# Sum of absolute differences by row: loads on one queue, absolute sums on ScalarE, last row in pieces

## Chip, cores and metric

The kernel runs on one core of a Trainium2 chip. The metric is the device time of one execution in microseconds (us), the median of three runs.

## What is computed

`x` and `y` are float32 matrices of 1024 rows and 4096 columns (16.78 MB each). The output holds, for each row, the sum over the columns of the absolute differences:

```python
def reference(x, y, axis):          # axis = -1
    return np.sum(np.abs(x - y), axis=axis).astype(np.float32)
```

## The kernel before

The 1024 rows are dealt to the 128 partitions, eight consecutive rows to each (`(p k) c -> p k c`). One step of the loop (line 29, `KCS = [1]*8`) takes one row of every partition: a tile `tx` of 128x4096 and a tile `ty` of the same shape, 2 MB each. In the text such a step is called a row, rows 0 to 7. Each step has four instructions:

- line 33: SP's queue loads `tx` from `x`; line 34: ScalarE's queue loads `ty` from `y`. ScalarE does nothing else.
- line 35: VectorE subtracts `ty` from `tx` in place.
- line 36: VectorE sums the absolute values of `tx` into one column of `ro` (128x8).

At the end line 38 stores `ro` (4 KB) on SP's queue. The pools `px1` and `py1` have four buffers each, so the first four rows are loaded at once, and the load of row k+4 waits until VectorE has finished with row k. The order of VectorE's instructions is set by the scheduler of the framework, not by the source: it often puts the subtractions of two rows ahead of their two sums (rows 1 and 2, 3 and 4, 5 and 6).

Of the kernel before, what the change touches and what calls it, by code (L numbers as in the profile page):

```python
# [5 lines left out]

KCS = [1]*8

@with_exitstack
def kernel(ctx, tc, x, y, axis, out):  # L10
    nc = tc.nc
    P = nc.NUM_PARTITIONS
    R, C = x.shape
    K = R // P
    xr = x.rearrange("(p k) c -> p k c", p=P, k=K)
    yr = y.rearrange("(p k) c -> p k c", p=P, k=K)
    orr = out.rearrange("(p k) -> p k", p=P, k=K)
    kcs = KCS
    assert sum(kcs) == K
    pools = {}  # L20
    for kc in set(kcs):
        pools[kc] = (
            ctx.enter_context(tc.tile_pool(name=f"px{kc}", bufs=4)),
            ctx.enter_context(tc.tile_pool(name=f"py{kc}", bufs=4)),
        )
    with tc.tile_pool(name="pr", bufs=1) as poolr:
        ro = poolr.tile([P, K], mybir.dt.float32)
        o = 0
        for kc in kcs:
            poolx, pooly = pools[kc]  # L30
            tx = poolx.tile([P, kc, C], x.dtype)
            ty = pooly.tile([P, kc, C], y.dtype)
            nc.sync.dma_start(out=tx, in_=xr[:, o:o+kc, :])
            nc.scalar.dma_start(out=ty, in_=yr[:, o:o+kc, :])  # L34
            nc.vector.tensor_sub(out=tx, in0=tx, in1=ty)  # L35
            nc.vector.reduce_sum(out=ro[:, o:o+kc], in_=tx, axis=mybir.AxisListType.X, apply_absolute_value=True)  # L36
            o += kc
        nc.sync.dma_start(out=orr, in_=ro)


# [1 line left out]
_INS = ['x', 'y', 'axis']  # L42
_OUTS = [((1024,), 'float32')]
#: Inputs that are plain numbers.
_NUMBERS = {'axis': -1}


def kernel(**inputs):
    import numpy as _np
    import concourse.bacc as _bacc  # L50
    import concourse.tile as _tile
    from concourse import mybir as _mybir
    from concourse.bass_utils import run_bass_kernel_spmd as _run

    nc = _bacc.Bacc("TRN2", target_bir_lowering=False, num_devices=1)  # L55
    arrays, args = {}, []
    for name in _INS:
        if name in _NUMBERS:
            args.append(_NUMBERS[name])
            continue  # L60
        a = _np.ascontiguousarray(inputs[name])
        if a.dtype.kind in "iu":
            a = a.astype(_np.int64)
        arrays[f"in_{name}_dram"] = a
        args.append(nc.dram_tensor(f"in_{name}_dram", a.shape, _mybir.dt.from_np(a.dtype), kind="ExternalInput").ap())
    for i, (shape, dtype) in enumerate(_OUTS):
        dt = _mybir.dt.from_np(_np.dtype(dtype))
        args.append(nc.dram_tensor(f"out_{i}_dram", shape, dt, kind="ExternalOutput").ap())
    with _tile.TileContext(nc) as tc:
        kernel(tc, *args)  # L70
    r = _run(nc, [arrays], core_ids=[0])
    got = tuple(r.results[0][f"out_{i}_dram"] for i in range(len(_OUTS)))
    return got[0]
```

## Time and profile before

| what | us |
|---|---|
| median of three runs (lowest, highest) | 97.6 (97.56, 97.62) |
| span of the profiled execution, first to last instruction | 95.8 |
| median less span: what lies around the span | 1.8 |
| VectorE busy in the span | 69.9 |

The profile is of one execution and gives its span; for the time of a run, what lies around the span has to be added. All times in the views are microseconds from the start of the span. The views used further down are the page's busy times and its forty slices, the table by stretches of time, the waits, the timeline, the chain that ended last, the groups of instructions and the transfers with their time from issue to landing.

### The profile page before, as it was taken

To read this page: it belongs to the slowest core of one execution; us is meant where nothing else is said; L and a number is where in the kernel's file an instruction comes from. 1 tells how busy PE (TensorE), PEld (TensorE's weight loads), DVE (VectorE), ACT (ScalarE), POOL (GpSimd) and SP (SyncE) were. 2 spreads that over 40 slices of the span, in tenths; PEclk is the share of its full clock that TensorE was granted. 3 is DMA by queue.
4 is the path that set the end of the run, shared out by engine and by line. 5 is a ranking of instruction groups with operands and counts; after the bars stand their busy time and mean duration, and the time that the engine had idled before them with its cause. 6 is when DMAs were issued, how large, how long until landed. Compare 5 with 4: busy or idle time off the path is not lost.

```text
span 95.8 us, 95 instructions
## 1 busy us (share of the span) xinstructions
DVE 69.9 (73%) x16; POOL 0.2 (0%) x4
## 2 busy tenths in 40 slices
DVE  0000069996930499999982999999909999999990
POOL 0000000000000000000000000000000000000000
DMA  4899999999999999999999999999999995000000
GB/s 109 369 431 424 424 438 438 438 431 438 431 424 438 424 417 431 431 411 431 438 438 424 431 431 431 424 424 424 431 411 438 438 438 212 0 0 0 0 0 2
DMA packets 2448, 33.56 MB, mean 350 GB/s; under 512 B 400, under 2 KB 400, under 8 KB 400
## 3 DMA queue, kind: packets, MB, share of 16 engines
q1 hardware_dynamic: 1296, 16.78, 41.7%
q10 hardware_dynamic: 1152, 16.78, 41.1%
HBM read 33.55 MB, written 0.00 MB: 350 GB/s over the span
## 4 chain that ended last, share of the span: by engine, by line
DMA 68%; DVE 24%; issue 4%; ACTq 1%
DMA ty<-in_y_dram 68%; DVE tx L35 14%; DVE ro L36 10%; ACTq L34 1%
## 5 line engine op out<-in xcount | busy, mean ns | idle before, releaser
L35 DVE TENSOR_TENSOR tx<-tx,ty 128x4096 f32<-128x4096 f32 x8 | 35.4, 4422 | 23.6 <-DMA ty<-in_y_dram 23.6
L36 DVE TENSOR_REDUCE ro<-tx 128x1 f32<-128x4096 f32 x8 | 35.1, 4413 | 0.1
L55 POOL MEMSET const-bfloat16-1.0<- 128x1 bf16 x1 | 0.1, 103 | 0.0
L55 POOL MEMSET const-uint8-127<- 128x1 uint8 x1 | 0.1, 103 | 0.0
L55 POOL MEMSET const-float32-1.0<- 128x1 f32 x1 | 0.1, 100 | 0.0
L55 POOL MEMSET const-float32-0.0<- 128x1 f32 x1 | 0.1, 99 | 0.2 <-issue 0.2
## 6 DMA issues: line engine op xcount, KB each, us to landing
ty<-in_y_dram ACTq DMA_DIRECT2D x8, 2048.0 KB, 33.1
tx<-in_x_dram SPq DMA_DIRECT2D x8, 2048.0 KB, 23.6
out_dram<-ro SPq DMA_DIRECT2D x1, 4.0 KB, 1.4
```

Of the source, the lines that this page charges most:

```text
L34: nc.scalar.dma_start(out=ty, in_=yr[:, o:o+kc, :])
L35: nc.vector.tensor_sub(out=tx, in0=tx, in1=ty)
L36: nc.vector.reduce_sum(out=ro[:, o:o+kc], in_=tx, axis=mybir.AxisListType.X, apply_absolute_value=True)
L55: nc = _bacc.Bacc("TRN2", target_bir_lowering=False, num_devices=1)
```

## The change

- All loads are issued by SP, x before y, row by row (lines 39 and 40). There are six buffers for x and six for y.
- Row 7 is loaded in four pieces of columns, `PIECES = [2304, 1152, 512, 128]`, each piece with a load of x and one of y (lines 44 and 45).
- For rows 0 to 6 VectorE subtracts (line 50) and ScalarE takes the absolute value and, in the same instruction, its sum into `ro` (line 51).
- For row 7, VectorE subtracts piece by piece (line 64), and ScalarE writes the absolute sums of the first three pieces to three columns of a small tile `last` (line 65). The difference of the last piece, 128 columns, is written beside these into `last` (line 67), and one VectorE sum over 131 columns gives row 7's result (line 68).
- The program runs in the order in which it is written (`manual_schedule`).

```diff
-KCS = [1]*8
+PIECES = [2304, 1152, 512, 128]
...
+    px = ctx.enter_context(tc.tile_pool(name="px", bufs=6))
+    py = ctx.enter_context(tc.tile_pool(name="py", bufs=6))
+    ps = ctx.enter_context(tc.tile_pool(name="ps", bufs=1))
+    with tc.manual_schedule():
+        ro = ps.tile([P, K], F32, tag="ro")
+
+        last = ps.tile([P, n_part + PIECES[-1]], F32, tag="last")
+        tiles = []
+
+        def load(k):
+            tx = px.tile([P, C], F32, tag="tx")
+            ty = py.tile([P, C], F32, tag="ty")
+            tiles.append((tx, ty))
+            if k < K - 1:
+                nc.sync.dma_start(out=tx, in_=xr[:, k, :])
+                nc.sync.dma_start(out=ty, in_=yr[:, k, :])
+                return
+            o = 0
+            for w in PIECES:
+                nc.sync.dma_start(out=tx[:, o:o + w], in_=xr[:, k, o:o + w])
+                nc.sync.dma_start(out=ty[:, o:o + w], in_=yr[:, k, o:o + w])
+                o += w
+
+        def whole(k):
+            tx, ty = tiles[k]
+            nc.vector.tensor_sub(out=tx, in0=tx, in1=ty)
+            nc.scalar.activation(tx, tx, ABS, accum_out=ro[:, k:k + 1])
+
+        for k in range(4):
+            load(k)
+        for k in range(K - 1):
+            if k + 4 < K:
+                load(k + 4)
+            whole(k)
+        tx, ty = tiles[K - 1]
         o = 0
-        for kc in kcs:
-            poolx, pooly = pools[kc]
-            tx = poolx.tile([P, kc, C], x.dtype)
-            ty = pooly.tile([P, kc, C], y.dtype)
-            nc.sync.dma_start(out=tx, in_=xr[:, o:o+kc, :])
-            nc.scalar.dma_start(out=ty, in_=yr[:, o:o+kc, :])
-            nc.vector.tensor_sub(out=tx, in0=tx, in1=ty)
-            nc.vector.reduce_sum(out=ro[:, o:o+kc], in_=tx, axis=mybir.AxisListType.X, apply_absolute_value=True)
-            o += kc
+        for i, w in enumerate(PIECES):
+            s = slice(o, o + w)
+            if i < n_part:
+                nc.vector.tensor_sub(out=tx[:, s], in0=tx[:, s], in1=ty[:, s])
+                nc.scalar.activation(tx[:, s], tx[:, s], ABS, accum_out=last[:, i:i + 1])
+            else:
+                nc.vector.tensor_sub(out=last[:, n_part:n_part + w], in0=tx[:, s], in1=ty[:, s])
+                nc.vector.reduce_sum(out=ro[:, K - 1:K], in_=last, axis=AX, apply_absolute_value=True)
+            o += w
         nc.sync.dma_start(out=orr, in_=ro)
```

The end of VectorE's program before: two subtractions, two sums, then row 7's subtraction and sum (L35 is the subtraction, L36 the sum; x2 are two in a row, of different rows).

```order
L35 TENSOR_TENSOR tx<-tx,ty 128x4096 x2
L36 TENSOR_REDUCE ro<-tx 128x1 x2
L35 TENSOR_TENSOR tx<-tx,ty 128x4096
L36 TENSOR_REDUCE ro<-tx 128x1
L69 UNCONDITIONAL_BRANCH
```

And the whole of VectorE's program in the change:

```order
L50 TENSOR_TENSOR tx<-tx,ty 128x4096 x7
L64 TENSOR_TENSOR tx<-tx,ty 128x2304
L64 TENSOR_TENSOR tx<-tx,ty 128x1152
L64 TENSOR_TENSOR tx<-tx,ty 128x512
L67 TENSOR_TENSOR last<-tx,ty 128x128
L68 TENSOR_REDUCE ro<-last 128x1
L101 UNCONDITIONAL_BRANCH
```

Nothing but subtractions stands ahead of row 7's pieces, and one sum behind them.

ScalarE's program, as one difference: eight loads of y go, a table load and ten activations come.

```order
-L34 DMA ty<-in_y_dram 128x4096 x8
-L69 UNCONDITIONAL_BRANCH
+L101 UNCONDITIONAL_BRANCH
+L51 ACT_TABLE_LOAD
+L51 ACTIVATE tx,ro<-tx 128x4096 x7
+L65 ACTIVATE tx,last<-tx 128x2304
+L65 ACTIVATE tx,last<-tx 128x1152
+L65 ACTIVATE tx,last<-tx 128x512
+L101 UNCONDITIONAL_BRANCH
```

The last three activations are those of row 7's first three pieces, behind the activation of row 6.

The end of SP's program in the change, from row 6's loads on, with the semaphores that each load waits for (DMAHW0 to DMAHW7 are given to the loads in turn, so a load waits for the one eight places ahead of it; Activation is ScalarE, DVE is VectorE):

```order
L39 DMA tx<-in_x_dram 128x4096 [waits DMAHW4_49,Activation_49]
L40 DMA ty<-in_y_dram 128x4096 [waits DMAHW5_49,DVE_49]
L44 DMA tx<-in_x_dram 128x2304 [waits DMAHW6_49,Activation_49]
L45 DMA ty<-in_y_dram 128x2304 [waits DMAHW7_49,DVE_49]
L44 DMA tx<-in_x_dram 128x1152 [waits DMAHW0_49]
L45 DMA ty<-in_y_dram 128x1152 [waits DMAHW1_49]
L44 DMA tx<-in_x_dram 128x512 [waits DMAHW2_49]
L45 DMA ty<-in_y_dram 128x512 [waits DMAHW3_49]
L44 DMA tx<-in_x_dram 128x128 [waits DMAHW4_49]
L45 DMA ty<-in_y_dram 128x128 [waits DMAHW5_49]
L70 DMA out_dram<-ro 128x8 [waits DMAHW6_49,DVE_49]
```

Before, SP issued eight loads of x and the store; now 22 loads and the store stand in one line.

## Rows read from the trace of the kernel before

**Rows 1.** The page: busy time by engine, and the DMA engines in forty slices.

```profile
span 95.8 us, 95 instructions
...
DVE 69.9 (73%) x16; POOL 0.2 (0%) x4
...
DVE  0000069996930499999982999999909999999990
...
DMA  4899999999999999999999999999999995000000
```

**Rows 2.** Stretches: start:end, length, DVE busy, POOL busy, PEclk, DMA share, GB/s.

```profile
0.00:2.00 2.00, 0.00 (x0) 0.20 (x4) 1.00 0.57 131
60.00:70.00 10.00, 9.51 (x3) 0.00 (x0) 1.00 1.00 424
70.00:75.00 5.00, 3.30 (x1) 0.00 (x0) 1.00 1.03 436
79.00:80.00 1.00, 1.00 (x1) 0.00 (x0) 1.00 1.00 426
80.00:81.00 1.00, 1.00 (x2) 0.00 (x0) 1.00 0.29 115
81.00:82.00 1.00, 1.00 (x1) 0.00 (x0) 1.00 0.00 0
```

**Rows 3.** The waits: engine, line, what for, us in total, times, longest.

```profile
DVE tx L35 <- DMA ty<-in_y_dram: 23.6, 5, 12.9
```

**Rows 4.** Timeline: start us, us, engine, line, operation, what it waited for.

```profile
12.92 4.43 DVE L35 TENSOR_TENSOR tx<-tx,ty 128x4096 f32<-128x4096 f32 x1 [12.92 <-DMA ty<-in_y_dram]
...
32.51 4.43 DVE L35 TENSOR_TENSOR tx<-tx,ty 128x4096 f32<-128x4096 f32 x1 [5.37 <-DMA ty<-in_y_dram]
...
71.70 4.43 DVE L35 TENSOR_TENSOR tx<-tx,ty 128x4096 f32<-128x4096 f32 x1 [2.19 <-DMA ty<-in_y_dram]
76.04 8.74 DVE L36 TENSOR_REDUCE ro<-tx 128x1 f32<-128x4096 f32 x2
84.70 4.42 DVE L35 TENSOR_TENSOR tx<-tx,ty 128x4096 f32<-128x4096 f32 x1
89.15 4.42 DVE L36 TENSOR_REDUCE ro<-tx 128x1 f32<-128x4096 f32 x1
93.60 0.35 SPq L38 DMA_DIRECT2D out_dram<-ro  x1
```

**Rows 5.** The chain that ended last, its last pieces: start us, us, what.

```profile
36.97 34.71 DMA ty<-in_y_dram
71.68 0.02 issue
71.70 4.43 DVE tx L35
76.13 5.22 DVE ro L36 x2
81.34 3.36 issue
84.70 4.43 DVE tx L35
89.13 0.02 issue
89.15 4.42 DVE ro L36
```

**Rows 6.** Groups of instructions: line, engine, operation, count, busy us, mean ns, idle before.

```profile
L35 DVE TENSOR_TENSOR tx<-tx,ty 128x4096 f32<-128x4096 f32 x8 | 35.4, 4422 | 23.6 <-DMA ty<-in_y_dram 23.6
L36 DVE TENSOR_REDUCE ro<-tx 128x1 f32<-128x4096 f32 x8 | 35.1, 4413 | 0.1
L55 POOL MEMSET const-uint8-127<- 128x1 uint8 x1 | 0.1, 103 | 0.0
```

**Rows 7.** Timeline of the start: the first four loads of each queue.

```profile
0.72 2.05 ACTq L34 DMA_DIRECT2D ty<-in_y_dram  x4
0.73 1.88 SPq L33 DMA_DIRECT2D tx<-in_x_dram  x4
```

**Rows 8.** The page's transfers: issues, KB each, median us from issue to landing; and queues.

```profile
q1 hardware_dynamic: 1296, 16.78, 41.7%
q10 hardware_dynamic: 1152, 16.78, 41.1%
...
ty<-in_y_dram ACTq DMA_DIRECT2D x8, 2048.0 KB, 33.1
tx<-in_x_dram SPq DMA_DIRECT2D x8, 2048.0 KB, 23.6
out_dram<-ro SPq DMA_DIRECT2D x1, 4.0 KB, 1.4
```

15 lines of the change are left out of this document (5 added, 10 removed).

## The prediction

> **What bounds the kernel now.** I began with the page's busy times and slices [rows 1]. VectorE is busy for 73% of the span, the DMA row reads 9 from the third slice to the 33rd and then drops to 0, while VectorE's row reads 9 to the end. So there are two stages: one in which the loads set the pace, and a tail in which VectorE works alone. The table by stretches [rows 2] gives the border: the DMA share is 1.00 at 424 GB/s between 60 and 70 us, still 1.00 between 79 and 80, 0.29 in the next microsecond, then 0.00.
>
> In the first stage VectorE waits for data: 23.6 us in five waits, all for y [rows 3]. The timeline [rows 4] shows the pace. Subtractions that start straight from such a wait start at 32.51 (row 2) and 71.70 (row 6), four rows apart: (71.70 - 32.51) / 4 = 9.80 us for each pair of 2 MB tiles. From row 0, at 12.92, six steps of 9.80 also give 71.7. Row 7's pair, which VectorE did not wait for, therefore lands at 71.70 + 9.80 = 81.50; that is an estimate, and it fits the stretch in which the DMA share falls to zero.
>
> The tail is the last piece of the chain [rows 5]. At 81.50 VectorE still owes the sums of rows 5 and 6, which its order put ahead of row 7's subtraction. That one starts at 84.70, 3.20 us after its data, and then come its 4.43 and the last sum's 4.42, to 93.57. From there to the end of the span, 95.8, are 2.23 us: the store's issue, its landing and the end of the program. The runs' median lies 1.8 above the profiled span, and I add that to every span below. A difference over 0.2% (0.2 us) counts as a difference.
>
> **The change part by part.**
>
> *The stream of loads.* The same 33.55 MB go through the same engines, at a share that is already 1.00. I keep 9.80 us a row and 71.70 as row 6's landing. Four SP issues take 1.88 us [rows 7], some 0.47 each; 22 of them need 10.3 us of SP's time in 81.5. The deeper buffers gain nothing, because no stretch between the start and 80 us shows engines without work. SP's line has one new danger: each load waits for the one eight places ahead of it. The last one, y's 128 columns, waits for y of row 6, which lands at 71.70. Its own turn in the stream comes at about 81.2, so 9.5 us cover an issue of 0.5. The waits on ScalarE ahead of rows 6 and 7 are for rows 0 and 1, done some 20 us earlier. If this cover were gone, the delay would go straight onto the last landing. Moving the y loads off ScalarE's queue costs nothing and keeps them from standing behind activations.
>
> *The sums that leave VectorE.* Eight sums of 4.41 us go [rows 6], 35.1 us in all. Six of them lay beside the loads and gain nothing. VectorE's subtraction of row 6 then ends at 71.70 + 4.43 = 76.13, and VectorE is free for row 7's pieces.
>
> *Row 7 in pieces.* By columns, 9.80 us split into 5.51, 2.76, 1.22 and 0.31: the pieces land at 77.21, 79.97, 81.19 and 81.50. A subtraction costs 4422 ns / 4096 = 1.08 ns a column [rows 6]. For a small operation's fixed part I add 0.10, the time of the 128x1 operation on POOL, the nearest small one [rows 6]. That gives 2.59, 1.34, 0.65 and 0.24 us. They run 77.21 to 79.80, 79.97 to 81.31, 81.31 to 81.96, and 81.96 to 82.20. The final sum over 131 columns is another 0.24.
>
> *The sums on ScalarE.* No row shows an activation, so I bound its price. At one end ScalarE is so quick that it is never last: the final sum then starts at 82.20 and ends at 82.44, the span at 84.67, the time is 86.5. At the other end it takes what VectorE takes for its sum of the same shape, 4.41 us for 4096 columns, in practice the subtraction's figures: row 6 from 76.15 to 80.57, then the pieces, 2.59, 1.34 and 0.65, one behind the other, to 85.15. The final sum ends at 85.39, the span at 87.62, the time is 89.4. ScalarE thus becomes the last link for any price but a very low one, since row 6's activation ends close to the last landing and 3968 columns wait behind it. Nothing in the rows decides between the ends, which lie 2.9 us apart; I take the middle, **88.0 us**, a gain of 9.6. Both ends stay in the range.
>
> The Trainium skill (ScalarE: Activation LUTs, section on the table load's cost) states 186 ns plus 0.833 ns an element for an activation. By that the passes would be 3.60, 2.11, 1.15 and 0.61 us, the last would end at 83.7, and the time would be 88.0 as an estimate; no row here shows it yet.
>
> The table load at the head of ScalarE's program is covered by the first landing and subtraction: the first activation can't start before 12.92 + 4.43 = 17.35 [rows 4].
>
> **The rivals.**
>
> *One queue does not stream (the other side).* If the engines drained one transfer of a queue before they began the next, each of the 21 boundaries between 22 transfers would cost a bubble. The gain of 9.6 is used up at 9.6 / 21 = 0.46 us a boundary; above that the change is slower. A cold start is dear: in the first 2 us the engines ran at 131 GB/s [rows 2], and row 0 was ready at 12.92, 3.1 us later than a pair needs in the stream. With 0.6 us a boundary, a fifth of this, 12.6 us would come on top: 100.6. In its mild form, 0.1 a boundary, the time is 90.1. For it: before, two queues always had work, 41.7% and 41.1% of the engines' span [rows 8], and one could fill the other's gap, so no row shows a queue alone. Against it: each queue had up to four transfers in flight, the one queue now has eight, and with the engines at a share of 1.00 nothing suggests that they wait for a transfer to be confirmed. I give 0.12 to the mild form and 0.03 to the dear one.
>
> *Small pieces do not stream.* The only small transfer in the trace, the store of 4 KB, took 1.4 us from issue to landing [rows 8]. If the last two pieces of 64 KB took 1.4 each, instead of 0.31 together, the last landing would be at 81.19 + 2.80 = 83.99. The last subtraction and the final sum would follow to 84.47, the time would be 88.5: the loads would be last, with ScalarE close beside. If all eight pieces put 1.4 on top of the stream, 11.2 us, the landing would be at 92.7 and the time at 97.2, hardly faster than before. For it: row 7 has 512-byte runs at its end. Against it: the pieces are issued ahead, so their way from issue to landing overlaps, and only what a small run costs an engine is left. Chance 0.05. The Trainium skill (DMA: Bandwidth & Descriptors, table of measured sizes) speaks against such pieces: it asks for 1 MiB or more and gives 0.95 us for 64 KB. Two such at the end would put the last landing at 83.1, an estimate, with a time of 87.6 by the loads' own path, which a ScalarE of the middle price covers; no row shows it.
>
> *ScalarE is slower than VectorE.* At r times VectorE's price its four last passes take 9.00 r us, and the time is 80.42 + 9.00 r. That is 91.2 at 1.2, and it passes the old time at 1.91, where a row takes 8.4 us. Since even then a row fits into the 9.80 of its loads, only the tail would show it. No row speaks for or against. Chance 0.05, nearly all below 1.91.
>
> **How the numbers follow.** My forecast (tail set by ScalarE, between 86.5 and 89.4) has 0.75. The range runs from 86.5, where ScalarE is hidden, to 90.0: it takes in the forecast's own spread, the low form of the small pieces, a ScalarE up to 6% slower than VectorE and about half of the mild bubbles. About 0.15 is left out, nearly all above. Faster by over 0.2%: 0.96. Slower: 0.03, the dear bubbles with a little of the slow ScalarE. Within 0.2%: 0.01, for the crossing points of these.
>
> **What would show it.** Right: the last landing near 81.5, subtractions of rows 0 to 6 that each wait for y and start about 9.8 apart, no idle time between the last activations, the final sum released by ScalarE and not by a load, and some 2.2 us behind it. The chain should be loads, one subtraction, four activations, the sum, the store. The pace of rows 0 to 6 tells the queue's part: over 9.80, and the first rival is at work. A gap between the subtractions of the last pieces with landings after 82 would be the second. ScalarE's mean for 128x4096 fixes the middle: 4.4 means 89.4, about 3.6 means 88. The forecast is wrong if the final sum ends before 82.4 or after 85.4, or if loads last beyond 82.5.

## The result and the profile after

The changed kernel takes 88.3 us, against 97.6 before: a ratio of 0.9045 (95% interval 0.9033 to 0.9058). The forecast was 88.0 in a range of 86.5 to 90.0.

The page of the changed kernel: busy times, and the span in forty slices.

```profile
span 86.6 us, 118 instructions
...
DVE 36.1 (42%) x12; ACT 31.2 (36%) x21; POOL 0.2 (0%) x4
...
DVE  0000009900495009910496008910396008949920
ACT  5000000097003930088003930088003940079970
...
DMA  3899999999999999999999999999999999999400
```

These lines answer to [rows 1]. VectorE's 69.9 us have become 36.1, and ScalarE has taken 31.2. The row to compare is the DMA's: before, a 5 and six slices without loads stood at its end, with VectorE busy in five of the six; now a 4 and two such slices stand there. The end has moved toward the last landing, not the landing toward the start.

The stretches of the changed kernel; its columns are those of [rows 2] with ACT busy behind DVE.

```profile
60.00:70.00 10.00, 4.42 (x1) 3.92 (x4) 0.00 (x0) 1.00 1.00 424
...
80.00:81.00 1.00, 0.77 (x1) 1.00 (x1) 0.00 (x0) 1.00 1.05 355
81.00:82.00 1.00, 0.98 (x2) 1.00 (x1) 0.00 (x0) 1.00 0.08 24
```

424 GB/s at a share of 1.00 between 60 and 70 us, as in [rows 2], from one queue in place of two. The small pieces show between 80 and 81: a share of 1.05 gives only 355 GB/s.

The timeline of the changed kernel from row 5 on.

```profile
61.99 4.42 DVE L50 TENSOR_TENSOR tx<-tx,ty 128x4096 f32<-128x4096 f32 x1 [5.36 <-DMA ty<-in_y_dram]
...
71.71 0.33 SPq L45 DMA_DIRECT2D ty<-in_y_dram  x1
71.81 4.43 DVE L50 TENSOR_TENSOR tx<-tx,ty 128x4096 f32<-128x4096 f32 x1 [5.40 <-DMA ty<-in_y_dram]
76.27 3.62 ACT L51 ACTIVATE tx<-tx 128x4096 f32<-128x4096 f32 x1 [6.11 <-DVE tx L50]
77.39 2.56 DVE L64 TENSOR_TENSOR tx<-tx,ty 128x2304 f32<-128x2304 f32 x1 [1.15 <-DMA ty<-in_y_dram]
79.80 0.19 ACT L51 ACTIVATION_READ_ACCUMULATOR tx<-tx 128x1 f32 x1
79.98 2.12 ACT L65 ACTIVATE tx<-tx 128x2304 f32<-128x2304 f32 x1
80.23 2.07 DVE L64 TENSOR_TENSOR tx<-tx,ty 128x1152 f32<-128x1152 f32 x2 [0.29 <-DMA ty<-in_y_dram]
...
82.10 1.15 ACT L65 ACTIVATE tx<-tx 128x1152 f32<-128x1152 f32 x1
82.22 0.28 DVE L67 TENSOR_TENSOR last<-tx,ty 128x128 f32<-128x128 f32 x1
...
83.25 0.61 ACT L65 ACTIVATE tx<-tx 128x512 f32<-128x512 f32 x1
...
83.98 0.29 DVE L68 TENSOR_REDUCE ro<-last 128x1 f32<-128x131 f32 x1 [1.48 <-ACT tx L65]
84.30 0.35 SPq L70 DMA_DIRECT2D out_dram<-ro  x1
```

Row 6's subtraction starts at 71.81, where it started at 71.70 before [rows 4]. Then ScalarE works from 76.27 to 83.96 without idle time: row 6, then the three pieces. VectorE is through with its last subtraction at 82.50 and waits 1.48 us for ScalarE before the final sum. The last load, issued at 71.71, landed 10.2 us later, at 81.9, so the loads were not last either. Its row in the view of transfers (KB, us from issue to landing):

```profile
ty<-in_y_dram SPq DMA_DIRECT2D x1, 64.0 KB, 10.2
```

From the end of the final sum, 84.27, to the end of the span are 2.33 us, 2.23 before.

### The profile page after: what moved, and what is told of

It reads as the page before. It is cut to its first block, busy times and chain, and to the rows that moved or that the text cites. A ratio compares the mean times of both kernels' runs of the same rounds, so it can differ in the third digit from the quotient of the medians.

```text
span 86.6 us, 118 instructions
## 1 busy us (share of the span) xinstructions
DVE 36.1 (42%) x12; ACT 31.2 (36%) x21; POOL 0.2 (0%) x4
## 2 busy tenths in 40 slices
DMA packets 3312, 33.56 MB, mean 388 GB/s; under 512 B 496, under 2 KB 752, under 8 KB 1264
## 3 DMA queue, kind: packets, MB, share of 16 engines
q1 hardware_dynamic: 3312, 33.56, 92.1%
## 4 chain that ended last, share of the span: by engine, by line
DMA 79%; ACT 9%; DVE 5%; SPq 3%; issue 1%; ACTq 0%; DVEq 0%
DMA ty<-in_y_dram 79%; DVE tx L50 5%; ACT tx L65 4%; ACT tx L51 4%; SPq L39 1%; SPq L40 1%; DVE ro L68 0%; ACTq L101 0%; DVEq L50 0%
## 5 line engine op out<-in xcount | busy, mean ns | idle before, releaser
L50 DVE TENSOR_TENSOR tx<-tx,ty 128x4096 f32<-128x4096 f32 x7 | 31.0, 4425 | 45.3 <-DMA ty<-in_y_dram 45.3
L51 ACT ACTIVATE tx<-tx 128x4096 f32<-128x4096 f32 x7 | 25.3, 3616 | 52.0 <-DVE tx L50 52.0
L64 DVE TENSOR_TENSOR tx<-tx,ty 128x2304 f32<-128x2304 f32 (+2 forms) x3 | 4.6, 1536 | 1.5 <-DMA ty<-in_y_dram 1.4
L65 ACT ACTIVATE tx<-tx 128x2304 f32<-128x2304 f32 (+2 forms) x3 | 3.9, 1294 | 0.0
L51 ACT ACT_TABLE_LOAD x1 | 1.3, 1283 | 0.7 <-PEq L87 0.7
L51 ACT ACTIVATION_READ_ACCUMULATOR tx<-tx 128x1 f32 x7 | 1.3, 186 | 0.0
L65 ACT ACTIVATION_READ_ACCUMULATOR tx<-tx 128x1 f32 x3 | 0.6, 187 | 0.0
```

The costliest lines, as they stand in the source:

```text
L51: nc.scalar.activation(tx, tx, ABS, accum_out=ro[:, k:k + 1])
L64: nc.vector.tensor_sub(out=tx[:, s], in0=tx[:, s], in1=ty[:, s])
L65: nc.scalar.activation(tx[:, s], tx[:, s], ABS, accum_out=last[:, i:i + 1])
```

## Experiments

Each kernel was timed beside the kernel before on the same chip. The first four take the change apart.

**The order alone.** The kernel before with VectorE's instructions in the written order, subtraction and sum of a row side by side; two queues and four buffers as before.

```diff
+    with tc.manual_schedule(), ...
...
+        for k in range(4):
+            load(k)
+        for k in range(K):
+            tx, ty = tiles[k]
             nc.vector.tensor_sub(out=tx, in0=tx, in1=ty)
+            nc.vector.reduce_sum(out=ro[:, k:k+1], in_=tx, ...)
+            if k + 4 < K:
+                load(k + 4)
```

> The kernel before with one difference: VectorE's order is written out, subtraction then sum for each row; two queues, four buffers, everything else as before. Theory (the old tail was VectorE's backlog): row 6 lands at 71.7, its sum ends at 80.5, row 7's subtraction starts at its landing, 81.5, and the last sum ends at 90.35, so the time is 94.4, 3.2 below the kernel before. Rival (the tail was bound by the loads, and what the change gained came from the deeper single queue): the order alone gives nothing, 97.6.

Measured: 94.36 us, ratio 0.9663 (0.9649 to 0.9678). Its timeline from row 6 on:

```profile
71.66 4.43 DVE L42 TENSOR_TENSOR tx<-tx,ty 128x4096 f32<-128x4096 f32 x1 [0.92 <-DMA ty<-in_y_dram]
76.12 4.42 DVE L43 TENSOR_REDUCE ro<-tx 128x1 f32<-128x4096 f32 x1
81.44 4.43 DVE L42 TENSOR_TENSOR tx<-tx,ty 128x4096 f32<-128x4096 f32 x1 [0.90 <-DMA ty<-in_y_dram]
85.90 4.42 DVE L43 TENSOR_REDUCE ro<-tx 128x1 f32<-128x4096 f32 x1
```

Row 7's subtraction now waits for its data and starts at 81.44, where before it started at 84.70 [rows 4]. So 3.2 of the 9.3 us come from the order alone. The row also confirms the landing of row 7, which the prediction had to work out (81.50) because no instruction of the kernel before waited for it.

**Without the pieces.** The change with row 7 loaded, subtracted and summed whole.

```diff
-            if k < K - 1:
+            if True:
...
-        tx, ty = tiles[K - 1]
...
+        whole(K - 1)
```

> The change without the pieces: row 7 is loaded, subtracted and summed whole. Theory: the pair lands at 81.6, the subtraction ends at 86.0 and ScalarE's pass at 89.8, then 2.3 and 1.7 behind it: 93.8. The pieces are then worth 5.5 of the 9.3 us. Rival (the new tail is ScalarE's backlog of whole rows, so that pieces hardly matter): under 91.

Measured: 93.61 us (0.9587, 0.9573 to 0.9601). The pieces are worth 5.3 us. ScalarE in place of VectorE for whole rows, with everything else of the change, is worth only 94.36 - 93.61 = 0.75: ScalarE's pass is the shorter by 0.8 us, and behind the last whole row the two engines work one after the other.

**Pieces without ScalarE.** The change with every sum on VectorE, right behind its subtraction.

```diff
-            nc.scalar.activation(tx, tx, ABS, accum_out=ro[:, k:k + 1])
+            nc.vector.reduce_sum(out=ro[:, k:k + 1], in_=tx, axis=AX, apply_absolute_value=True)
...
-                nc.scalar.activation(tx[:, s], tx[:, s], ABS, accum_out=last[:, i:i + 1])
+                nc.vector.reduce_sum(out=last[:, i:i + 1], in_=tx[:, s], axis=AX, apply_absolute_value=True)
```

> The change with all sums on VectorE, each behind its subtraction, pieces and loads as in the change; ScalarE does nothing. Theory (pieces pay only where a second engine takes the sums): from row 6's landing at 71.8 VectorE has two rows of 8.85 us and the pieces' fixed parts to do without a gap, to 90.2, and the time is 93.9 to 94.4, as with whole rows in written order (94.4). Rival (pieces bring their 5.3 us by themselves, since the work behind the last landing is small): about 89.

Measured: 94.14 us (0.9648, 0.9632 to 0.9664). The same pieces that bring 5.3 us with ScalarE bring 0.2 without it. Two rows of its timeline:

```profile
71.80 4.43 DVE L50 TENSOR_TENSOR tx<-tx,ty 128x4096 f32<-128x4096 f32 x1 [0.91 <-DMA ty<-in_y_dram]
...
80.59 2.55 DVE L64 TENSOR_TENSOR tx<-tx,ty 128x2304 f32<-128x2304 f32 x1
```

From 71.80 on VectorE never waits, so the pieces can save it no more than the 0.9 us that it waits beside the loads of a row. In the change, where ScalarE takes the sums, this wait is 5.40 us, and the pieces bring 5.3. Neither the pieces nor the second engine gains much alone. Together they let the tail follow the landings.

**Four equal pieces.** `PIECES = [1024, 1024, 1024, 1024]`.

> The change with four equal pieces of 1024 columns. Theory (ScalarE's backlog from row 6 on sets the end, so the last piece's size has slack): ScalarE ends its third piece at 83.1, VectorE its last subtraction at 82.8, the final sum over 1027 columns takes 1.2 and ends at 84.3 to 84.5, the time is 88.3 to 88.6. Rival (the work behind the last landing sets the end, which is what shrinking pieces are for): 896 more columns in the last subtraction and the last sum, at 1.05 ns each, 1.9 us more, 90.2.

Measured: 88.50 us (0.9063, 0.9050 to 0.9077), which the interval hardly parts from the change. The end of its timeline:

```profile
81.73 1.04 ACT L65 ACTIVATE tx<-tx 128x1024 f32<-128x1024 f32 x1
81.77 1.22 DVE L67 TENSOR_TENSOR last<-tx,ty 128x1024 f32<-128x1024 f32 x1 [1.31 <-DMA ty<-in_y_dram]
82.68 0.19 ACT L65 ACTIVATION_READ_ACCUMULATOR tx<-tx 128x1 f32 x1
83.10 1.22 DVE L68 TENSOR_REDUCE ro<-last 128x1 f32<-128x1027 f32 x1
```

The time is in the theory's range, but the last link is the one that the rival named: VectorE's own work behind the last landing ends the program, at 84.32; in the change ScalarE's backlog did, at 84.27. VectorE's last subtraction and sum take 1.9 us more than with 128 columns, but ScalarE, which leaves 1024 columns to VectorE in place of 128, is done at 82.87 in place of 83.96. The final sum so starts 0.88 us earlier, and its added 0.93 is all that is lost. Row 6's subtraction also started earlier in this run (71.58, in the change 71.81); counted from there, the equal pieces lose 0.28 us. So the shrinking widths are not where the gain is.

**ScalarE's pass over row 6 twice.**

```diff
             whole(k)
+            if k == K - 2:
+                tx, ty = tiles[k]
+                nc.scalar.activation(tx, tx, ABS, accum_out=ro[:, k:k + 1])
```

> The change with ScalarE's pass over row 6 made twice, the second one directly behind the first with the same result. Theory (from row 6 on ScalarE is the last link without slack): the whole pass of 3.71 us shows, 92.0. Rival (loads and VectorE end last, ScalarE has slack): less than half of it shows, under 90.

Measured: 91.94 us (0.9424, 0.9408 to 0.9439), 3.6 above the change for a pass of 3.62: from row 6 on ScalarE has no slack to speak of. The second pass and the one behind it:

```profile
79.95 3.62 ACT L61 ACTIVATE tx<-tx 128x4096 f32<-128x4096 f32 x1
...
83.57 2.11 ACT L68 ACTIVATE tx<-tx 128x2304 f32<-128x2304 f32 x1
```

From the start of a whole row's pass to the start of the next are 3.62 us where the next has its data; the theory's 3.71 held a short wait (see the part on the prediction).

**Both queues.** The y loads of rows 0 to 6 issued by ScalarE, row 7's by SP.

```diff
-                nc.sync.dma_start(out=ty, in_=yr[:, k, :])
+                nc.scalar.dma_start(out=ty, in_=yr[:, k, :])
```

> The change with the y loads of rows 0 to 6 issued by ScalarE, row 7's pieces as in the change. Theory (a queue alone streams as well as two): the same pace of 9.80 a row, and 88.3 within 0.3. Rival (a boundary between transfers costs something on one queue, which two hide): up to 1 us faster at 0.05 us a boundary.

Measured: 88.27 us (0.9048, 0.9026 to 0.9070), no difference. One queue streams as well as two.

**All y loads on ScalarE's queue**, row 7's pieces too.

```diff
-                nc.sync.dma_start(out=ty[:, o:o + w], in_=yr[:, k, o:o + w])
+                nc.scalar.dma_start(out=ty[:, o:o + w], in_=yr[:, k, o:o + w])
```

> The change with all y loads, row 7's pieces too, issued by ScalarE in the program's order. Theory (a queue of an engine that computes holds its work back): the pieces' issues stand ahead of row 3's pass and wait for the transfers eight places ahead, the last for y of row 6 at 71.7; ScalarE then has four passes of 3.71 and the pieces' 4.0 to do, the final sum ends at about 91, the time is 95. Rival (these waits are covered): 88.3.

Measured: 95.27 us (0.9761, 0.9747 to 0.9776), 7.0 slower than the change. Two of its timeline's rows:

```profile
61.71 10.68 ACTq L45 DMA_DIRECT2D ty<-in_y_dram  x4
...
72.44 3.62 ACT L51 ACTIVATE tx<-tx 128x4096 f32<-128x4096 f32 x1 [31.71 <-DMA ty<-in_y_dram]
```

Four issues of y pieces, each held back for a transfer eight places ahead, stand in front of ScalarE's pass over row 3. That pass starts at 72.44, after 31.71 us of idle time; in the change it starts at 46.87. The loads themselves are on time: the first piece's subtraction starts at 77.48, in the change at 77.39. The kernel with both queues lost nothing by issues of whole rows on ScalarE's queue: there each issue waits for a row that the pass behind it needs too. The prediction had feared loads that stand behind activations; the loss comes from activations that stand behind loads. What the single queue brings is that no engine that computes issues loads.

**Four buffers in place of six**, with the load of row k+4 behind the work on row k.

> The change with four buffers for x and four for y; a load waits for ScalarE and VectorE to be done with the row four ahead. Theory (the deeper buffers gain nothing): ScalarE is done with row 0 at 21.1, when three rows are still to come from transfers already issued, so no engine of the DMA runs dry: 88.3 within 0.2. Rival (the six buffers carry part of the gain): a pace over 9.80 a row, 89 or more.

Measured: 88.25 us (0.9051, 0.9029 to 0.9074). The deeper buffers bring nothing.

**Row 7 in 32 loads**, the work in the pieces of the change. A run is what a load moves to one partition in one stretch; a load has 128 runs, eight for each of the 16 engines. (The views of transfers count 2448 packets for the 17 transfers before and 3312 for the 23 of the change: 144 for each, of which 128 are the runs.)

```diff
-            for w in PIECES:
+            for w in [256] * 16:
```

> The change with row 7 loaded in 16 pieces of 256 columns each for x and y (32 loads of 128 KB in place of eight); subtractions and sums keep the pieces of the change. Theory (a piece costs the engines a little for each of its runs, nothing for being a transfer of its own): the change's eight loads put its last landing about 0.4 us behind the stream's pace with 48 more runs an engine; 240 more runs make 1.5 to 2.1 us, the first piece's subtraction ends at about 81.2, ScalarE at 85.1, and the time is 89.0 to 89.5. Rival (each small transfer pays its own way, 1.4 us as the store did): 32 times 1.4 in place of 9.8 put 35 us on top, 123.

Measured: 92.11 us (0.9436, 0.9422 to 0.9450). The rival is far off, but the theory is off too, by 2.6 us. The timeline of SP's issues shows why, and then the stretches:

```profile
72.03 0.43 SPq L44 DMA_DIRECT2D tx<-in_x_dram  x1
72.50 0.43 SPq L45 DMA_DIRECT2D ty<-in_y_dram  x1
72.98 0.43 SPq L44 DMA_DIRECT2D tx<-in_x_dram  x1
...
82.94 0.43 SPq L45 DMA_DIRECT2D ty<-in_y_dram  x1
```

```profile
60.00:70.00 10.00, 4.43 (x1) 3.91 (x4) 0.00 (x0) 1.00 1.00 428
...
72.00:74.00 2.00, 2.00 (x1) 0.00 (x0) 0.00 (x0) 1.00 1.11 348
...
78.00:80.00 2.00, 0.25 (x1) 1.93 (x2) 0.00 (x0) 1.00 0.87 269
80.00:82.00 2.00, 2.00 (x1) 0.00 (x0) 0.00 (x0) 1.00 0.87 265
```

SP issues one load after the other at 0.47 us each, from 72.03 to 82.94, without a wait between them. 128 KB (131 KB in thousands) each 0.47 us are 276 GB/s, and that is what flows once the loads issued earlier are used up. I had counted the cost of the runs, which shows alone between 72 and 74 (348 GB/s), and left out the issue: with eight loads in flight and each of them small, SP can't work ahead.

**Row 7 in 16 loads** tells the two apart: these are issued in less time than they take.

```diff
-            for w in PIECES:
+            for w in [576] * 6 + [512, 128]:
```

> The change with row 7 loaded in six pieces of 576 columns, one of 512 and one of 128 (16 loads in place of eight); work in the change's pieces. Theory (a run of its own costs an engine about 9 ns, and the loss of the 32 loads came from SP's issue at 0.47 us each, slower than 128 KB need): 16 loads are issued in 7.6 us, within the 9.8 of the row, so only the runs show, 64 more by 9 ns or 0.5 us, and the time is 88.6 to 88.9. Rival (each load more costs about 0.16 us, as 3.8 us over 24 loads gave): 89.5 or more.

Measured: 88.91 us (0.9114, 0.9100 to 0.9127), 0.6 above the change, at the upper end of the theory's 88.6 to 88.9. Eight loads more are 64 runs more for each engine, so by the time a run costs 0.6 / 64, some 9.4 ns. By the engines' rate it is less: between 72 and 74 us they move 391 GB/s in place of 424, which is 0.06 us more for a load of 288 KB, or 7 ns a run. No step of 0.16 us a load is seen, which would have made 89.6. Every load here has 128 runs, so a cost of the run and a cost of 0.06 to 0.08 us for the load can't be told apart. The delay enters with the first piece, now eight loads: ScalarE waits for its subtraction.

```profile
80.48 2.12 ACT L65 ACTIVATE tx<-tx 128x2304 f32<-128x2304 f32 x1 [0.64 <-DVE tx L64]
```

**Row 6 in halves.** Two halves of row 6, summed into two columns and added by a VectorE sum of two columns, and row 7 in five pieces.

```diff
-PIECES = [2304, 1152, 512, 128]
+HALVES = [2048, 2048]
+PIECES = [1792, 1152, 640, 384, 128]
...
+        for i, w in enumerate(HALVES):
+            s = slice(o, o + w)
+            nc.vector.tensor_sub(out=tx[:, s], in0=tx[:, s], in1=ty[:, s])
+            nc.scalar.activation(tx[:, s], tx[:, s], ABS, accum_out=six[:, i:i + 1])
+            o += w
```

> The change with row 6 also cut, into two halves of 2048 columns (loads, subtractions and ScalarE's sums, added up by a small VectorE sum), and row 7 in pieces of 1792, 1152, 640, 384 and 128. Theory: row 6's activations end at about 76.1 in place of 80.0, so that the first piece's pass starts when its subtraction ends, 78.3, and the pieces follow their landings: the final sum ends at 83.4 in place of 84.3, the time is 87.4. Rival (the tail is the work behind the last landing and the finer cuts only add fixed parts): 88.3 to 88.8.

Measured: 87.56 us (0.8971, 0.8957 to 0.8984). And with the pieces 1792, 1024, 640, 384 and 256:

> Row 6 in halves, row 7 in pieces of 1792, 1024, 640, 384 and 256. Theory: the pass of the piece of 384 starts some 0.3 us earlier than with 1152, ..., 128, and the last piece's subtraction and sum cost 0.27 more in place of waiting 0.48 for ScalarE: 87.2 to 87.5, against 87.56. Rival (VectorE's last two instructions now set the end): 87.6 to 87.9.

Measured: 87.31 us (0.8948, 0.8934 to 0.8961). Both beat the change; the intervals of the two overlap by a little, so which widths are better isn't settled. The end of the second one's timeline:

```profile
74.31 1.91 ACT L68 ACTIVATE tx<-tx 128x2048 f32<-128x2048 f32 x1 [2.21 <-DVE tx L67]
...
78.45 1.70 ACT L78 ACTIVATE tx<-tx 128x1792 f32<-128x1792 f32 x1 [2.14 <-DVE tx L77]
78.93 1.23 DVE L77 TENSOR_TENSOR tx<-tx,ty 128x1024 f32<-128x1024 f32 x1 [0.51 <-DMA ty<-in_y_dram]
...
82.23 0.53 ACT L78 ACTIVATE tx<-tx 128x384 f32<-128x384 f32 x1
82.30 0.43 DVE L80 TENSOR_TENSOR last<-tx,ty 128x256 f32<-128x256 f32 x1
...
82.89 0.42 DVE L81 TENSOR_REDUCE ro<-last 128x1 f32<-128x260 f32 x1 [0.16 <-ACT tx L78]
```

ScalarE now waits for VectorE and VectorE for the loads, and VectorE waits only 0.16 us for ScalarE before the final sum. The final sum ends at 83.31; the change's ended at 84.27.

## Why the prediction was right

The groups of instructions of the changed kernel, shapes apart, answer to [rows 6]:

```profile
L50 DVE TENSOR_TENSOR tx<-tx,ty 128x4096 f32<-128x4096 f32 x7 | 31.0, 4425 | 45.3 <-DMA ty<-in_y_dram 45.3
L51 ACT ACTIVATE tx<-tx 128x4096 f32<-128x4096 f32 x7 | 25.3, 3616 | 52.0 <-DVE tx L50 52.0
...
L51 ACT ACTIVATION_READ_ACCUMULATOR tx<-tx 128x1 f32 x7 | 1.3, 186 | 0.0
L51 ACT ACT_TABLE_LOAD x1 | 1.3, 1283 | 0.7 <-PEq L87 0.7
...
L64 DVE TENSOR_TENSOR tx<-tx,ty 128x512 f32<-128x512 f32 x1 | 0.7, 693 | 0.0
L65 ACT ACTIVATE tx<-tx 128x512 f32<-128x512 f32 x1 | 0.6, 613 | 0.0
```

- **The stream** kept its pace: rows 5 and 6 start 71.81 - 61.99 = 9.82 apart, 9.80 forecast, and two queues give the same time. The last landing, 81.9, was forecast at 81.5: 0.1 of the difference is row 6's later landing, and some 0.3 are what the pieces cost the engines, which I had put at nothing in the sum. ScalarE's backlog covers nearly all of it.
- **The tail is ScalarE's.** This was the step on which the forecast stood, and the wait of 1.48 us before the final sum, the doubled pass and the idle-free row of activations show it. The price I had to bound lay between nothing and 4.42 us a row; it is 3.62. From row 6's pass to the next are 79.98 - 76.27 = 3.71, because the next had to wait for VectorE: its subtraction of the first piece ended at 79.95. (The read of row 6's sum lies beside this wait, so the view shows no idle time.) In the kernel with both queues that subtraction ended at 79.77, and the pass began 3.62 after row 6's. By the forecast's middle the final sum would have ended at 83.92; it ended at 84.27. Of these 0.35 us, 0.12 is row 6's pass, which started at 76.27 and not at 76.15; 0.16 lies in ScalarE's four passes (7.69 in place of 7.53), of which 0.09 is this wait; and 0.07 is the final sum and its release. The store's end took 0.1 more and what lies around the span 0.1 less. That the middle came so close is luck: the rows gave the two ends and that ScalarE would end last between them, and nothing in them decided where.
- **VectorE's price** was a little low for the small pieces: 693 ns for 512 columns against 0.65, 290 for the final sum against 0.24. From 4425 ns for 4096 columns and 693 for 512, a column costs 1.04 ns and the fixed part is 0.16 us; I had 1.08 and 0.10, the latter from another engine.
- **The cover of SP's line** held: the last load was issued at 71.71, ten microseconds ahead of its landing. The kernel with 32 loads shows what happens when SP can't issue ahead: it is 3.8 us slower, of which the runs alone (192 more an engine at 7 to 9.4 ns) would have made 1.4 to 1.8. The waits on ScalarE ahead of rows 6 and 7 were also covered, but by 6.5 us and not by some 20: row 0's sum was done at 21.21, and row 6's first load was issued at 27.72.
- **The rivals.** No bubble is seen between transfers of one queue. Small pieces stream: the store's 1.4 us is not paid by each. ScalarE is the faster of the two engines for this sum. The mild bubble was priced too high: by the forecast's own path ScalarE would have covered the eight boundaries behind row 6, and the 13 ahead of it make 89.3 at 0.1 each, not 90.1.
- **The old tail.** At 81.50 VectorE owed only the rest of row 6's sum; row 5's had ended at about 80.5 [rows 4]. The 3.20 us up to row 7's subtraction stand.

The Trainium skill (ScalarE: Activation LUTs, section on the table load's cost) has 186 ns plus 0.833 ns an element; the rows of 3616 and 613 ns agree with its 3.60 and 0.61 us. Its four passes, added up from 76.15, would have ended at 83.6 as an estimate, not at 83.7 as the prediction has it. The table load's row, 1283 ns at 0.73 us, lies well ahead of the first activation at 17.50. By an estimate from the Trainium skill's table of measured sizes (DMA: Bandwidth & Descriptors, section on bandwidth), which is for loads issued from GpSimd, two pieces of 64 KB would have put the last landing at 83.1. The trace differs: it came at 81.9, and these pieces had been issued ten microseconds ahead.

## What to carry to other kernels

When loads set the pace, look at the work that is owed at the last landing: here the sum of a whole row, put ahead of the last row by an order that nobody wrote down, was 3.2 of the 9.3 us. Cutting the last row pays as far as the engine behind the loads has time to spare beside them: VectorE alone waited 0.91 us a row and the pieces brought 0.2, with ScalarE beside it 5.40 and they brought 5.3. So give the stages to two engines first, and then cut the row before it too, as soon as the last engine still owes it. Issue loads that may have to wait from a queue whose engine does not compute, and in few enough pieces that the issue stays ahead of the DMA engines.

## What was not expected

- SP's issue limits a row of 32 loads: 0.47 us each, 276 GB/s for 128 KB, where the engines could take 348.
- ScalarE's sum comes with an instruction of its own, a read of the accumulator of 186 ns, which the order of the program does not list. About half of it lies beside the next activation where that one has its data.
- A shrinking last piece, 128 columns in place of 1024, was worth no more than 0.2 to 0.3 us in this kernel, and the intervals of the two times overlap.
